# Matmul groups of the projection, gate and MLP stages draw their PSUM banks from more pools

## The chip, the cores and the metric

One core of one Trainium2 chip. The metric is the device time of one execution in microseconds; the median of three runs is compared. TensorE is PE below (its weight loads PEld), VectorE DVE, ScalarE ACT, GpSimd POOL, and SyncE, which issues every DMA, SP.

## What is computed

A sequence of 1024 tokens with 1024 features goes through two kinds of block, all in fp32.

```python
# first block, once
x = x + concat([diff_attention, neighbourhood_attention]) @ w_out
x = x + sigmoid(x @ w_ple_gate) * (p @ w_ple_proj)
# second block, layers l = 0, 1
mod = silu(c) @ w_mod[l] + b_mod[l]              # six rows of shifts, scales and gates
x = x + gt1 * (concat([dilated, latent_attention]) @ w_out_2[l])
h = rms_norm(x) * (1 + sc2) + sh2
x = x + gt2 * (square(relu(h @ w_mlp_in[l])) @ w_mlp_out[l])
```

## The kernel before

Activations are held transposed, features on partitions: a tile is 128 features by 512 tokens, and the two halves of the tokens are `half` 0 and 1. Every fp32 matrix is split into a high and a low part (`h`, `l`), and a product of a 128-feature step is three matmuls of 128x512 (`mm3`, L183 to L185; `product`, L1709). A matmul group accumulates into one PSUM bank and is then read once by DVE or ACT.

**The eight banks** belong to pools: `psG` (2 banks, tile `pg`), `psS` (2, scores, `sps`), `psA` (1, attention values, `pa`), `psT` (2, transposes, `pt`) and `psJ` (1, transposes, `pj`). A new tile of a pool waits until the reader of the tile that had the bank is done.

**The stages around the change**, by the time from the span's start:

- End of the first block, 760 to 1000 (`block1_end`). The output projection (`out_proj`) makes 16 products of 24 matmuls, for two feature tiles d by half 0, then half 1, for four pairs of d. Each is added to the old x on DVE (L872; `xo` is loaded by a DMA, two buffers), and the sum is split by ACT (L127) and DVE (L128) into the tiles a00 to a71, from which the gate's 16 products read: all eight of a half for every product. The gate's bank is read by ACT (tanh, L919), DVE adds (L920, L921). `side()` interleaves two other pieces of work: position tables (DVE L1156, `tab`, two buffers, each stored by a DMA to `acd`), and the modulation's matrix-vector sums (`mod_piece`: a DMA load `modraw`, DVE L969 into `macc`, transposes on PE into `pt` or `pj`, L161, L974).
- The output projections of the layers, near 1585 to 1700 and 3040 to 3172 (L874), behind the latent attention.
- MLP up, near 1740 to 2070 and 3200 to 3505. A feature group `fg` makes seven products of 12 matmuls (a form of Strassen's scheme): `up_first` opens x (bank S) and y (G), `up_rest` goes on with x and opens z (G). x stays open over the whole group, 19 us.
- MLP down, near 2070 to 2390 and 3515 to 3820: seven chunks `c` of two groups `dp` (`down_proj`). A group has seven products i of six matmuls for each of two columns j: x (S) takes i = 0, 2, 4, 6, y (G) i = 1 and another y i = 3, 5. After each product DVE adds the bank to x (L1831, `add_to`), so the next product into the same bank waits for that read. `u_parts` makes the chunk's operands (POOL L1812, POOL and DVE L1079, ACT L1078), `wide` its weights (a DMA load `sraw`, POOL L1684 to L1688 sums, ACT L1697, DVE and POOL L1698). The last of eight chunks is a plain product (`gemm_t`) of 16 groups.

**Order.** All engines run in order. The order of each engine's instructions is made by a list scheduler that simulates the program: among instructions that are ready in its simulation, a free bank included, it takes the one written first. So an engine's order is fixed before the run, and a bank that is free in the simulation lets a later product move ahead.

Of the kernel before, what the change touches and what calls it, by code (L numbers as in the profile page):

```python
# [11 lines left out]
F32 = mybir.dt.float32  # L12
# [6 lines left out]
P = 128  # L19
# [67 lines left out]
class Emit:  # L87
# [56 lines left out]
    def psum_g(self, shape=None):  # L144
        return self.psG.tile(shape or [P, 512], F32, tag="G", name="pg")

    def psum_s(self, shape=None):
        return self.psS.tile(shape or [P, 512], F32, tag="S", name="sps")

# [83 lines left out]
    def setup(self):  # L233
        nc = self.nc
        es = self.es
        self.dram = self.pool("dram", es, space=DRAM)
        self.const = self.pool("const", es)
        self.psS = self.pool("psS", es, {"S": 2}, PSUM)
        self.psA = self.pool("psA", es, {"A": 1}, PSUM)
        self.psT = self.pool("psT", es, {"T": 2}, PSUM)  # L240
        self.psJ = self.pool("psJ", es, {"J": 1}, PSUM)
        self.turn, self.apart = 0, False
        self.psG = self.pool("psG", es, {"G": 2}, PSUM)
        self.hp = self.pool("hp", es)
        self.wp = self.pool("wp", es, {"wh": WB, "wl": WB, "raw": 2})
        self.wring = [self.wp]
        self.st = self.pool("st", es, {"l1": 3, "l2": 3, "r24": 2, "rsy": 2, "rst": 2, "sr": 2, "stw": 2, "stc": 2, **{t: 4 for t in ("mn", "cc", "ssq", "r8")}})
        c = self.const
        self.ident = c.tile([P, P], F32, name="ident")
        make_identity(nc, self.ident)  # L250
        self.inv24 = c.tile([P, 24], F32, name="inv24")
        nc.vector.memset(self.inv24[:, 0:16], 1.0 / 64)
        nc.vector.memset(self.inv24[:, 16:24], 1.0 / 32)
        self.zeros = c.tile([P, 1], F32, name="zeros")
        nc.vector.memset(self.zeros, 0.0)
        self.mixd = [self.dram.tile([8, P, S], F32, name=f"mixd{b}") for b in range(3)]
        self.xTd = [self.dram.tile([8, P, S], F32, name=f"xTd{b}") for b in range(3)]
        self.xTm = self.dram.tile([8, P, S], F32, name="xTm")
        self.modd = {}
# [602 lines left out]
    def out_proj(self, w, b, gate, order, after, step=lambda: None, done=lambda d, half: None, pair=True):  # L862
        nc = self.nc

        def mul(d, half, wt, c0):
            sl = slice(half * 512, half * 512 + 512)
            xo = self.xt.tile([P, 512], F32, tag="xo", name="xo")
            self.dma(xo, self.xTd[b][d, :, sl])
            ps = self.psum_g()
            self.gemm_t(ps, self.mix, half, wt, 8, c0, order)  # L870
            if gate is None:
                nc.vector.tensor_tensor(self.X(d, half), ps, xo, op=OP.add)  # L872
            else:
                nc.vector.scalar_tensor_tensor(self.X(d, half), ps, gate[:, d:d + 1], xo, op0=OP.mult, op1=OP.add)  # L874
                self.dma(self.xTm[d, :, sl], self.X(d, half))
            done(d, half)

        self.halves(w, mul, after, step, self.first_w, pair)
# [9 lines left out]
    def block1_end(self, after):  # L888
        nc = self.nc
        x1 = self.act()  # L890

        def split_x(d, half):
            hi, lo = self.act_tile(x1, d, half)
            self.split(hi, lo, self.X(d, half))

        es = ExitStack()
        self.mod_pool = False
        self.mp = self.pool("mp2", es, {"mraw": 3})
        self.wring = [self.wp] * WB + [self.pool("gw", es, {"wh": 2, "wl": 2})] * 2
        self.mraw = (self.mp, "mraw")  # L900
        pp = self.pool("ple", es, {"gth": 3, "pl": 3})
        tables = self.position_tables(es)
        per = -(-len(tables) // 16)

        def side():
            for _ in range(min(per, len(tables))):
                tables.pop(0)()
            self.run_background(3)

        self.out_proj(self.A["w_out"][0], 0, None, None, lambda half: None, side, split_x, False)  # L910

        def mul(d, half, wt, c0):
            sl = slice(half * 512, half * 512 + 512)
            pl = pp.tile([P, 512], F32, tag="pl", name="ple")
            self.dma(pl, self.pled[d, :, sl])
            ps = self.psum_g()
            self.gemm_t(ps, x1, half, wt, 8, c0)
            th = pp.tile([P, 512], F32, tag="gth", name="gth")
            nc.scalar.activation(th, ps, AF.Tanh, scale=0.5)  # L919
            nc.vector.scalar_tensor_tensor(th, th, 1.0, pl, op0=OP.add, op1=OP.mult)  # L920
            nc.vector.tensor_tensor(self.X(d, half), self.X(d, half), th, op=OP.add)  # L921
            self.dma(self.xTd[1][d, :, sl], self.X(d, half))

        self.halves(self.A["w_ple_gate"][0], mul, after, side)
        self.wring = [self.wp]
        es.close()
# [792 lines left out]
    def mlp(self, l, close, after):  # L1719
# [18 lines left out]
            self.dma(ud[n, :, half * 512:half * 512 + 512], r)  # L1738

        def up_first(fg, w, pool, tag="r"):  # L1740
            x, y = self.psum_s(), self.psum_g()
            self.product(x, w, self.B, 0, slice(0, P), 4, True)
            t = keep(x)
            self.product(y, w, self.B, 1, slice(0, P), 4, True)
            put(2 * fg, 0, y, t, pool, tag)
            return x

        def up_rest(fg, w, x, up):
            mul = lambda ps, i, start: self.product(ps, w, self.B, i, slice(0, P), 4, start)
            z = self.psum_g()  # L1750
            mul(x, 2, False)
            t = keep(x)
            mul(z, 3, True)
            t5 = keep(z)
            mul(x, 4, False)
            put(2 * fg + 1, 1, x, t5, up)
            mul(z, 5, False)
            put(2 * fg, 1, z, t, up)
            mul(x, 6, False)
            put(2 * fg + 1, 0, x, None, up)  # L1760
# [72 lines left out]
        def down_proj(c, dp, B):  # L1833
            w = wide(A["w_mlp_out_2"][l], 4 * c, 2, dp * 512, 512)
            q = []
            for j in range(2):
                q.append((self.psum_s(), slice(j * P, (j + 1) * P), 4 * dp + j, 4 * dp + j + 2))
            y = {}
            for i in range(7):
                for j, (x, cols, d1, d2) in enumerate(q):  # L1840
                    if i in (1, 3):
                        y[j] = self.psum_g()
                    ps = y[j] if i in (1, 3, 5) else x
                    self.product(ps, w, B, i, cols, 2, i in (0, 1, 3))
                    for d, half in (((d1, 0),), ((d1, 0),), ((d1, 1),), ((d2, 1),), ((d2, 1),), ((d1, 1),), ((d2, 0),))[i]:
                        add_to(d, half, ps)
# [9 lines left out]
        with ExitStack() as eu:  # L1856
            up = self.pool("ud", eu, {"uq": 4})
            self.XT = {}
            B = u_parts(0, up)
            for d in (0, 2, 1, 3, 4, 6, 5, 7):  # L1860
                self.XT[d, 0], self.XT[d, 1] = self.slot(16 + d, F32)
                for half in range(2):
                    self.dma(self.X(d, half), self.xTm[d, :, half * 512:half * 512 + 512])
            for c in range(7):
                down_proj(c, 0, B)
                down_proj(c, 1, B)
                if c < 6:
                    B = u_parts(c + 1, up)
            U = {}
            for half in range(2):  # L1870
                for k in range(4):
                    u = up.tile([P, 512], F32, tag="uq", name="ul")
                    self.dma(u, ud[28 + k, :, half * 512:half * 512 + 512])
                    U[k, half] = hi, lo = self.slot(((14, 15, 24, 25), (26, 27, 8, 9))[half][k])
                    nc.scalar.copy(hi, u)
                    V.tensor_tensor(lo, u, hi.bitcast(F32), op=OP.subtract)
            wts = [self.load_w(A["w_mlp_out_2"][l, 28 * P:32 * P], [(dp * 512, 512)], 4) for dp in range(2)]
            for half in range(2):
                for d in range(8):
                    ps = self.psum_g()  # L1880
                    self.gemm_t(ps, U, half, wts[d // 4], 4, (d % 4) * P)
                    add_to(d, half, ps)
                    if l == 0:
                        self.dma(self.xTd[2][d, :, half * 512:half * 512 + 512], self.X(d, half))
                after(half)
# [80 lines left out]
```

## Time and profile before

| | us |
|---|---|
| median of three runs | 3882.95 (3879.51 to 3885.87) |
| profiled execution | 3880.11 |
| its span, first to last instruction | 3878.2 |
| PE busy in the span | 3613.2 (93%) |
| DVE busy | 2821.6 (73%) |
| POOL busy | 1565.9 (40%) |

The profiled execution ran 2.8 us below the median, and 1.9 us of it lie around the span. "Busy" is the union of an engine's instructions. In a view of waits, `PE pg L183 <- DVE xT L872` reads: PE's instruction of line 183 that writes `pg` stood idle until DVE's instruction of line 872 that writes `xT` was done. PEld waits are mostly the same idle time seen on the weight load.

### The profile page before, as it was taken

How to read it: one execution, taken by the hardware profiler on the slowest of the kernel's cores; microseconds unless marked ns; L12 is line 12 of the kernel's file. 1: busy time of each engine (PE TensorE's matmuls, PEld its weight loads, DVE VectorE, ACT ScalarE, POOL GpSimd, SP SyncE). 2: the span in 40 equal slices, each digit the busy share in tenths (PEclk: the TensorE clock that was granted, in tenths of full speed). 3: DMA queues.
4: the chain of work that ended last, by engine and by line, in shares of the span. 5: the costliest groups of instructions: out<-in, count | busy, mean ns of one | idle time of the engine just before them, and what ended most of it. 6: DMA issues, size and time to landing. Idle time of an engine off the chain costs nothing.

```text
span 3878.2 us, 59074 instructions
## 1 busy us (share of the span) xinstructions
PE 3613.2 (93%) x20508; PEld 3097.2 (80%) x20508; DVE 2821.6 (73%) x6304; ACT 1842.2 (48%) x3671; POOL 1565.9 (40%) x1317
## 2 busy tenths in 40 slices
PE   7999899989899899988998999899899998998999
PEld 6988899768899888777786777899788776886777
DVE  5888877667666788658889986666788646447885
ACT  4555555623455678533333333455677633333331
POOL 2334222322322223235337895422133235339882
PEclk9999999999899999999999999999999999999999
DMA  6322323575445500224555323455500132334322
GB/s 193 100 76 74 81 75 83 152 254 183 120 143 152 161 11 25 65 94 144 187 185 193 114 90 108 124 142 156 159 14 26 53 106 101 109 122 147 104 93 82
DMA packets 374077, 446.17 MB, mean 115 GB/s; under 512 B 50037, under 2 KB 246532, under 8 KB 373780
## 3 DMA queue, kind: packets, MB, share of 16 engines
q1 hardware_dynamic: 373780, 442.41, 36.7%
q8 instruction: 162, 2.65, 0.3%
q14 instruction: 135, 1.11, 0.1%
HBM read 312.17 MB, written 101.54 MB: 107 GB/s over the span
## 4 chain that ended last, share of the span: by engine, by line
PE 59%; DVE 16%; POOL 8%; DMA 8%; issue 5%; ACT 4%; SPq 1%; DVEq 0%; ACTq 0%; POOLq 0%
PE pg L183 8%; PE pg L184 8%; PE pg L185 8%; PE sps L1709 8%; PE pg L1709 6%; PE sps L459 2%; PE pt L155 2%; PE pt L693 2%; PE sps L460 2%; DVE macc L969 2%; PE sps L183 2%; DMA modraw<-in_w_mod_dram 2%; PE sps L184 2%; PE pa L700 2%; PE sps L185 2%
## 5 line engine op out<-in xcount | busy, mean ns | idle before, releaser
L209 POOL TENSOR_TENSOR wl<-raw,wh 128x512 fp32r<-128x512 f32 (+2 forms) x234 | 302.5, 1304 | 578.0 <-ACT wh L208 492.7
L128 DVE TENSOR_TENSOR pl<-pt,ph 128x512 fp32r<-128x512 f32 (+3 forms) x406 | 267.6, 665 | 85.8 <-ACT ph L127 77.3
L127 ACT CAST ph<-pt 128x512 fp32r<-128x512 f32 (+3 forms) x406 | 226.0, 574 | 136.1 <-PE pt L693 52.3
L208 ACT CAST wh<-raw 128x512 fp32r<-128x512 f32 (+2 forms) x234 | 138.1, 611 | 221.4 <-DMA raw<-in_w_out_dram 69.5
L969 DVE SCALAR_TENSOR_TENSOR macc<-modraw,csil,macc 128x256 f32<-128x256 f32 x280 | 205.3, 733 | 47.9 <-DMA modraw<-in_w_mod_dram 43.2
L459 PE MATMUL sps<-ks,qs 128*128 128x512 f32 (+3 forms) x480 | 195.8, 410 | 18.5 <-DVE mn L493 10.3
L1698 DVE TENSOR_TENSOR wl<-ssum,wh 128x1024 fp32r<-128x1024 f32 x116 | 168.6, 1453 | 47.5 <-ACT wh L1697 47.5
L1697 ACT CAST wh<-sraw 128x1024 fp32r<-128x1024 f32 x116 | 97.0, 836 | 221.8 <-PE sps L1709 121.4
L1684 POOL TENSOR_TENSOR ssum<-sraw 128x512 f32<-128x512 f32 x58 | 79.0, 1362 | 288.6 <-DVE wl L1698 122.7
L407 POOL TENSOR_TENSOR qn<-qn,r 128x512 f32<-128x512 f32 x64 | 68.8, 1080 | 266.5 <-DVE r L122 109.6
L460 PE MATMUL sps<-kl,qs 128*128 128x512 f32 (+3 forms) x480 | 175.4, 367 | 0.0
L1697 ACT CAST wh<-ssum 128x1024 fp32r<-128x1024 f32 x116 | 121.4, 1047 | 108.9 <-PE pg L1709 79.4
L1643 ACT ACTIVATE xm<-xm,mn 128x1024 f32<-128x1024 f32 x128 | 148.4, 1159 | 32.6 <-DVE mn L493 32.5
L493 DVE CUSTOM_DVE_ANT_0 xd<-sps,dtab 128x256 f32<-128x256 f32 (+1 forms) x256 | 103.3, 412 | 80.1 <-PE sps L460 72.0
L459 PEld LDWEIGHTS sps<-ks,qs 128*128 128x128 f32 x480 | 108.2, 225 | 28.5 <-DVE mn L493 15.0
L1698 POOL TENSOR_TENSOR wl<-sraw,wh 128x512 fp32r<-128x512 f32 x58 | 87.4, 1507 | 90.0 <-ACT wh L1697 81.4
L1698 DVE TENSOR_TENSOR wl<-sraw,wh 128x1024 fp32r<-128x1024 f32 x58 | 94.4, 1628 | 32.0 <-ACT wh L1697 23.9
L700 PE MATMUL pa<-pl,vpm 128*128 128x512 f32 x256 | 109.2, 427 | 2.9 <-DVE pl L128 2.7
L460 PEld LDWEIGHTS sps<-kl,qs 128*128 128x128 f32 x480 | 110.8, 231 | 1.3
L699 PE MATMUL pa<-ph,vpm 128*128 128x512 f32 x256 | 109.2, 427 | 0.6 <-ACT ph L127 0.2
L493 DVE CUSTOM_DVE_ANT_0 xm<-sps,zeros,mn 128x512 f32<-128x512 f32 x128 | 95.3, 745 | 13.8 <-PE sps L185 12.3
L693 PE MATMUL pt<-ident,xm 128*128 128x128 f32 x688 | 104.6, 272 | 0.6 <-DVE pl L128 0.6
(1483 smaller groups left out, 13960.6 us busy)
## 6 DMA issues: line engine op xcount, KB each, us to landing
modraw<-in_w_mod_dram SPq DMA_DIRECT2D x192, 256.0 KB
ud<-r SPq DMA_DIRECT2D x128, 256.0 KB
sraw<-in_w_mlp_in_dram SPq DMA_DIRECT2D x60, 512.0 KB
sraw<-in_w_mlp_out_dram SPq DMA_DIRECT2D x56, 512.0 KB
raw<-in_w_in_dram SPq DMA_DIRECT2D x194, 128.0 KB
uq<-ud SPq DMA_DIRECT2D x96, 256.0 KB
ks<-khh SPq DMA_DIRECT2D x128, 128.0 KB
dtab<-awd SPq DMA_DIRECT2D x32, 512.0 KB
```

The source lines that it names most:

```text
L127: nc.scalar.copy(hi, src)
L128: nc.vector.tensor_tensor(lo, src, hi.bitcast(F32), op=OP.subtract)
L183: nc.tensor.matmul(ps, lh, rh, start=start, stop=False)
L184: nc.tensor.matmul(ps, lh, rl, start=False, stop=False)
L185: nc.tensor.matmul(ps, ll, rh, start=False, stop=stop)
L209: nc.gpsimd.tensor_tensor(wl[:, sl], raw, wh[:, sl].bitcast(F32), op=OP.subtract)
L459: nc.tensor.matmul(ps, self.Q[m][:, q], self.K[m][:, k], start=True, stop=False)
L460: nc.tensor.matmul(ps, self.Q[m][:, q], self.KL[m][:, k], start=False, stop=True)
L969: nc.vector.scalar_tensor_tensor(acc, raw[:, k], c, acc, op0=OP.mult, op1=OP.add)
L1697: nc.scalar.copy(wh[:, 0:m], x)
L1698: (nc.vector if i < 3 else nc.gpsimd).tensor_tensor(wl[:, 0:m], x, wh[:, 0:m].bitcast(F32), op=OP.subtract)
L1709: nc.tensor.matmul(ps, x[:, k, cols], y, start=start and k + n == 0, stop=(k, n) == (nk - 1, 2), skip_group_check=True)
```

## The change

The matmul groups of six places no longer take a fixed pool but the next of a turn: output projections, gate and the last MLP chunk G, S, G, S, A (`psum_w()`); x of the MLP S, S, T; y and z of the MLP G, G, A. The counters run on over the whole program. No instruction is added or removed, and the pools keep their sizes. The `plain` products at the head of the MLP keep S and G.

```diff
+    def psum_w(self, turn="GSGSA"):
+
+        n = self.wide[turn] = self.wide.get(turn, -1) + 1
+        return {"G": self.psum_g, "S": self.psum_s, "A": self.psum_a, "T": self.psum_one}[turn[n % len(turn)]]()
+
+    def psum_one(self):
+        return self.psT.tile([P, 512], F32, tag="T", name="pt")
...
-        self.turn, self.apart = 0, False
+        self.turn, self.apart, self.wide = 0, False, {}
...
@@ out_proj
-            ps = self.psum_g()
+            ps = self.psum_w()
             self.gemm_t(ps, self.mix, half, wt, 8, c0, order)
...
@@ block1_end (the gate)
-            ps = self.psum_g()
+            ps = self.psum_w()
             self.gemm_t(ps, x1, half, wt, 8, c0)
...
@@ mlp: up_first, up_rest
-            x, y = self.psum_s(), self.psum_g()
+            x, y = self.psum_w("SST"), self.psum_w("GGA")
...
-            z = self.psum_g()
+            z = self.psum_w("GGA")
...
@@ mlp: down_proj
-                q.append((self.psum_s(), slice(j * P, (j + 1) * P), 4 * dp + j, 4 * dp + j + 2))
+                q.append((self.psum_w("SST"), slice(j * P, (j + 1) * P), 4 * dp + j, 4 * dp + j + 2))
...
-                        y[j] = self.psum_g()
+                        y[j] = self.psum_w("GGA")
...
@@ mlp: the last chunk
-                    ps = self.psum_g()
+                    ps = self.psum_w()
                     self.gemm_t(ps, U, half, wts[d // 4], 4, (d % 4) * P)
```

## Rows read from the trace of the kernel before

**Rows 1.** Busy time by stage; columns: PE, PEld, DVE, ACT, POOL busy, clock, DMA.
```profile
760.00:883.00 123.00, 105.15 (x452) 84.85 (x451) 85.45 (x164) 35.29 (x62) 31.03 (x24) 0.93 0.74 238
883.00:1000.00 117.00, 106.53 (x497) 88.57 (x496) 86.08 (x177) 39.11 (x64) 37.24 (x30) 0.94 0.51 165
1585.00:1700.00 115.00, 112.51 (x550) 91.78 (x549) 48.73 (x96) 46.15 (x80) 33.86 (x29) 1.00 0.33 108
...
3230.00:3515.00 285.00, 282.83 (x1244) 233.51 (x1243) 138.63 (x141) 101.49 (x146) 121.30 (x87) 1.00 0.40 135
3515.00:3820.00 305.00, 276.12 (x1155) 215.44 (x1155) 246.89 (x277) 105.07 (x153) 262.19 (x173) 0.99 0.29 97
```

**Rows 2.** Waits from 760 to 890; then DVE's groups from 760 to 883.
```profile
DVE tab L1156 <- DMA acd<-tab: 23.1, 14, 4.4
...
PE pg L183 <- DVE xT L872: 16.2, 5, 7.8
...
L1156 DVE SCALAR_TENSOR_TENSOR tab<-cmult,ac 128x512 f32<-128x512 f32 x32 | 25.7, 810 | 25.0 <-DMA acd<-tab 23.1 <-ACT ac L1151 1.7
L872 DVE TENSOR_TENSOR xT<-pg,xo 128x512 f32<-128x512 f32 x16 | 10.9, 682 | 0.9 <-DMA xo<-xTd 0.9
```

**Rows 3.** Timeline, projection to gate: DVE (L128), then PE (L183).
```profile
872.98 0.68 DVE L128 TENSOR_TENSOR a70l<-xT,a70h 128x512 fp32r<-128x512 f32 x1
...
886.19 1.78 DVE L128 TENSOR_TENSOR a71l<-xT,a71h 128x512 fp32r<-128x512 f32 x1
...
879.25 0.39 PE L183 MATMUL pg<-a00h,wh 128*128 128x512 f32 x1
...
890.38 0.39 PE L183 MATMUL pg<-a01h,wh 128*128 128x512 f32 x1
...
895.82 0.39 PE L183 MATMUL pg<-a01h,wh 128*128 128x512 f32 x1
```

**Rows 4.** PE's timeline behind one wait for a bank; the clock of two stretches.
```profile
860.93 0.50 PE L183 MATMUL pg<-a00h,wh 128*128 128x512 f32 x1 [1.97 <-DVE xT L872]
...
864.18 0.63 PE L184 MATMUL pg<-a30l,wh 128*128 128x512 f32 x1
864.61 0.63 PE L185 MATMUL pg<-a30h,wl 128*128 128x512 f32 x1
...
820.00:830.00 10.00, 7.74 (x28) 5.93 (x27) 7.05 (x10) 1.24 (x2) 3.71 (x3) 0.83 0.70 215
...
860.00:870.00 10.00, 9.07 (x34) 7.30 (x35) 9.82 (x19) 5.09 (x9) 2.73 (x2) 0.83 0.83 264
```

**Rows 5.** PE's idle moments at layer 0's projection, and at the second layer's head.
```profile
1628.49 0.66 PE L155 MATMUL pt<-ident,oT 128*128 128x128 f32 x4 [0.68 <-ACT oT L702]
1630.26 0.74 PE L183 MATMUL pg<-a60h,wh 128*128 128x512 f32 x2 [0.67 <-ACT a60h L127]
1632.74 0.50 PE L183 MATMUL pg<-a01h,wh 128*128 128x512 f32 x1 [0.39 <-DVE xT L874]
...
2435.72 0.36 PE L183 MATMUL pg<-wh,a00h 128*128 128x256 f32 x1 [0.95 <-DVE b22l L1831]
```

**Rows 6.** Waits of five down chunks, 3569.8 to 3787.7; busy time of one.
```profile
POOL ssum L1684 <- DMA sraw<-in_w_mlp_out_dram: 20.4, 5, 6.0
...
PE sps L1709 <- DVE b16h L1831: 11.4, 5, 2.4
...
3613.78:3656.90 43.12, 40.26 (x169) 32.34 (x169) 35.18 (x41) 15.27 (x23) 39.89 (x27) 0.96 0.30 94
```

**Rows 7.** Chain of work inside that chunk: start, length, what.
```profile
3631.17 1.26 POOL wl L1698
...
3632.45 0.38 SPq L108
...
3632.88 4.77 DMA sraw<-in_w_mlp_out_dram
...
3637.81 1.32 POOL ssum L1684
```

**Rows 8.** PE's timeline where the wait of rows 6 arises.
```profile
3607.18 0.39 PE L1709 MATMUL pg<-a21h,wh 128*128 128x512 f32 x1
...
3609.91 0.39 PE L1709 MATMUL sps<-a01h,wh 128*128 128x512 f32 x1
...
3613.78 0.79 PE L1709 MATMUL sps<-a41h,wh 128*128 128x512 f32 x1 [2.36 <-DVE b16h L1831]
```

**Rows 9.** DVE reading both pools' banks at L1831; PE's wait for weights, layer 0 up.
```profile
L1831 DVE SCALAR_TENSOR_TENSOR b16h<-pg,mod,b16h x16: 737/750/751, 2071.8 to 3825.6; 128x512 f32<-128x512 f32 x16
...
L1831 DVE SCALAR_TENSOR_TENSOR b16h<-sps,mod,b16h x14: 737/739/742, 2069.9 to 3786.9; 128x512 f32<-128x512 f32 x14
...
PE sps L1709 <- ACT wh L1697: 2.1, 1, 2.1
```

## The prediction

> **What bounds the kernel now.** I read the busy time by stage first, because the change touches only some stages and each has its own limit [rows 1]. Three kinds show. In MLP up of layer 1 PE is busy 282.83 of 285 us: there is nothing for a bank to free. In the projection of layer 0 it is 112.51 of 115. In the end of the first block (105.15 of 123) and in MLP down (276.12 of 305) PE has idle time, 18 and 29 us. So the question is who ends those idle stretches, and the waits answer it.
>
> In the end of the first block PE's one large wait is for a bank: 16.2 us in five waits of line 183 for the add of line 872 that reads the bank [rows 2]. Two banks hold two finished products, and DVE is late with its adds. It is late because it runs in order and stands 23.1 us before the tables of L1156, whose two buffers are still being stored. DVE itself hardly waits for PE or for anything else at its adds: 0.9 us before L872. The stage is thus paced by DVE and the table stores; PE's wait is the result.
>
> In MLP down the most visible PE wait comes once per chunk, 11.4 us in five, for the add into b16h [rows 6]. The plan put the products of y (a21) ahead of those of x, since x's bank was still taken; so i = 2 of x (a41) comes right behind i = 0 (a01) and must wait for its read, 2.36 us [rows 8]. It looks like a bank shortage. But POOL is busy 39.89 of that chunk's 43.12 us, and what idles it is its own loop: its L1698 releases the weight buffer, SP issues the load, it takes 4.77 us, and POOL's L1684 starts behind it [rows 7]. That wait is 20.4 us in five chunks [rows 6]. PE is not in that loop.
>
> **The change part by part.** No instruction is added, so the sum has only waits and order in it. DVE reads a bank of G in 750 ns and one of S in 739 at the same line [rows 9]; I take 0 for the change of pool, between 11 ns less and 11 more per read, and the same for T and A, which this line never reads now.
>
> *End of the first block.* With five banks PE may run up to four products past the last unread one. A product takes 895.82 - 890.38 = 5.44 us [rows 3], so three more banks are 16 us more of lead than now, more than any single wait (7.8 the longest), and all 16.2 us of waiting for L872 can go. What is late next is DVE. The gate needs all of half 0's splits, and the last, a70l, ends at 872.98 + 0.68 = 873.7; PE starts the gate at 879.25 [rows 3]. If DVE does the same work in the same order, the first product of the gate can end at 874.4 (three matmuls behind a70l), the second at 874.4 + 5.4 = 879.8, and the third waits for a71l at 886.19 + 1.78 = 888.0 and ends at 888.7. Before, it ended at 895.8. From there PE runs on as before. **Gain 7.1 us**, out of 16.2. The bounds: 0, if the gate's own DVE work, 86.08 of 117 us [rows 1], gives it back; and if the plan also brings the adds forward on DVE, all 16.2 plus the slow matmuls behind the waits. After the 1.97 us wait PE's matmuls come 0.43 us apart, the 1.2 GHz level, where a product's 24 in 5.44 us are 0.227 apart, the 2.4 GHz level [rows 3, 4]. Some 15 such matmuls cost 3 us, and two stretches of the stage have the mean clock 0.83 [rows 4], so 6: 22 us in all. SP's queue is not changed by itself: each product still issues one `xo` load behind the add two before it, and those adds come no later. The weights of the next pair need buffers that PE frees, and it frees them earlier.
>
> *Layer projections.* At the end of latent attention PE stands 0.68, 0.67 and 0.39 us [rows 5]. The last is for a bank and goes. In the first two a third product could be started, but its fourth step needs the same a60h. I take half of 1.35: 1.1 us a layer, 2.2 in both, between 0 and 3.5. That the first product of layer 1 draws A, which the last attention values hold, costs nothing while G and S products can be moved ahead of it.
>
> *Head of the second layer.* The 0.95 us wait for the bank that L1831 reads [rows 5] goes, since the last chunk's groups now lie in G, S and A: 1.0 us, between 0 and 1.
>
> *MLP up.* 0: PE has no idle time in layer 1 [rows 1]. What hides the reads of one bank there are the products into the others; if that cover were gone, each read would cost PE some 0.75 us [rows 9].
>
> *MLP down.* With T for x the next group's i = 0 need not wait for the last group's read, the pulled order of rows 8 goes, and with it PE's 2.36 us. I count 0: while POOL paces the chunk, PE then waits for POOL's operands instead. The bounds are the rival below, and the same amount lost if the new order suits POOL worse.
>
> Sum: 7.1 + 2.2 + 1.0 = 10.3 us. Against the profiled execution 3880.1 - 10.3 = 3869.8; the median lies 2.8 us above that execution, so **3872 us**, 0.28% less. A measurement of this kernel tells about 0.2%, 7.8 us, from no change.
>
> **A rule weighed.** In the down chunks the trace shows the same PE gap in each chunk and a POOL that is 92% busy [rows 6]. The Trainium skill's page Perfetto Trace Analysis, section Identifying Performance Opportunities, says that a gap which repeats on the engine that should be saturated can mean that there is not enough SBUF or PSUM for the next tile. By it the change would win the gap itself, which is the first rival; by the row the gap only shows POOL's pace.
>
> **The rivals.**
>
> *The down gap was worth its length.* If the planner, no longer short of banks, also orders POOL, ACT and DVE better, each of ten steady chunks could lose up to POOL's idle time, 43.12 - 39.89 = 3.2 us, and one and a half more where the clock falls behind the wait (0.96 in that chunk, 4% of 43 us = 1.7). At 2.3 to 4 us a chunk: 23 to 40 us, so 3832 to 3849. For it: DVE's late add sits behind its own weight splits, whose order the plan decides. Against it: rows 7. Chance 0.2.
>
> *DVE takes it all.* The tables and modulation sums move with the adds, the gate's start stays at 879, and only the small terms are left: 3880 to 3883. For it: DVE does not wait for PE today. Against it: PE starts the gate 5.6 us after its last operand of half 0 is ready, which is PE's own lateness. Chance 0.2.
>
> *Slower: PE stands before weights in MLP up.* With three banks for x the plan can pull the next group's first product ahead of the present group's last ones. PE is in order: if its weights land later than the plan thinks, everything of the present group stands behind it. The one such wait now is 2.1 us, for ACT's split [rows 9]. If it comes in 10 of 28 groups (the third that holds T), that is 21 us lost, less the 10 gained: 3893. It decides from a lateness of more than the product that is passed over, 2.7 us of cover. Against it: PE waits for weights once in layer 0's stage and hardly in layer 1, so they come with time to spare. Chance 0.15.
>
> **How the numbers follow.** My forecast has 0.45 and its own range is 3862 to 3880 (the bounds 22 + 4.5 and 0, with most near DVE's unchanged order). Faster by over 0.2% means under 3875.2: two thirds of the forecast's case (0.30), the down rival (0.20) and a little of the DVE rival (0.04): 0.54. Slower means over 3890.7: most of the slower rival, a little less the cases where its waits are short: 0.14. The rest, 0.32, is the same. The range runs from 3840, inside the down rival, to 3888, leaving out the ends of both.
>
> **What would show it.** Right: in the profile after, no wait of PE for L872; the gate's first matmul near 870 to 875 and its third product ending near 889; PE's idle time before the gate now put down to L128 or L127; the down chunks still 43 us long with POOL near 40 busy, the b16h wait gone or moved to POOL's parts. Wrong: chunks of 41 us or less (the first rival), the gate's third product still ending near 896 (the second), or new PE waits for L1697 or L1698 in MLP up with its groups longer than 19 us (the third).

## The result and the profile after

The changed kernel takes 3906.69 us in the median of four runs (3905.58 to 3910.88), the kernel before 3882.56 us beside it: ratio 1.0064, 95% interval 1.0047 to 1.0081, 24 us slower. The forecast was 3872. The profiled execution has a span of 3905.6 us where it was 3878.2. In the changed kernel's rows every line number above 150 is 8 higher (the bank's add of L872 is L880, the product's matmul L1709 is L1717, the macc of L969 is L977).

First, where the 27.4 us arise. I followed marks that both traces have. The end of the first block (ACT's last tanh) moves from 971.5 to 972.0, the first `keep` of layer 0's MLP up from 1731.6 to 1732.7: nothing yet. The `keep` copies that bracket MLP up of layer 0 then tell it. Of the kernel before, in a view by tile (engine, out and in, count: shortest/median/longest ns, first to last start):

```profile
L1727 ACT COPY keep<-sps x30: 561/589/590, 1731.6 to 2053.7; 128x512 f32<-128x512 f32 x30
L1727 ACT COPY keep<-pg x15: 572/578/592, 1773.1 to 2061.2; 128x512 f32<-128x512 f32 x15
```

And of the changed kernel:

```profile
L1735 ACT COPY keep<-sps x20: 562/584/611, 1732.7 to 2087.2; 128x512 f32<-128x512 f32 x20
...
L1735 ACT COPY keep<-pt x10: 571/580/589, 1813.2 to 2105.9; 128x512 f32<-128x512 f32 x10
L1735 ACT COPY keep<-pa x5: 583/590/594, 1822.2 to 2106.4; 128x512 f32<-128x512 f32 x5
```

The stage grew from 329.6 to 373.7 us, 44 us, more than the whole loss. From its end to the first keep of layer 1 the changed kernel gets back 14 us (1117.9 where it was 1132.0); MLP up of layer 1 is as long as before (312.0 and 310.8); from its end to the span's end it gets back 5 (369.3 and 374.2). With the 1.1 us of the beginning: 1 + 44 - 14 + 1 - 5 = 27.

What ended PE's idle time there stands in PE's waits from 1735 to 2115. Kernel before (us in total, times, longest):

```profile
PE pj L155 <- DVE macc L969: 8.8, 3, 4.7
...
PE pt L155 <- DVE macc L969: 2.3, 1, 2.3
PE sps L1709 <- ACT wh L1697: 2.1, 1, 2.1
```

Changed kernel:

```profile
PE pt L163 <- DVE macc L977: 26.7, 5, 11.2
PE sps L1717 <- ACT wh L1705: 6.3, 6, 2.1
...
PE pj L163 <- DVE macc L977: 4.1, 2, 2.4
...
PE sps L1717 <- DVE wl L1706: 3.1, 4, 1.6
```

The new wait is not one of a product at all. It is the transposes of the modulation sums into `pt`, standing before their macc. The timeline of PE at the longest one shows why products suffer (start, length, what, idle before it):

```profile
1878.36 0.39 PE L1717 MATMUL pg<-a70h,wl 128*128 128x512 f32 x1
1878.59 0.38 PE L163 MATMUL pt<-ident,macc 128*128 128x128 f32 x2
1890.14 0.66 PE L163 MATMUL pt<-ident,macc 128*128 128x128 f32 x2 [11.18 <-DVE macc L977]
1890.45 0.78 PE L1717 MATMUL pt<-a00h,wh 128*128 128x512 f32 x1
1891.03 0.63 PE L1717 MATMUL pt<-a00l,wh 128*128 128x512 f32 x1
1891.45 0.63 PE L1717 MATMUL pt<-a00h,wl 128*128 128x512 f32 x1
```

Directly behind the second sum comes the first product of a group whose x lies in T. The same order, a sum in T directly ahead of an x in T, stands at 1963.18 and 2039.40, where PE waits 3.02 and 9.70 us for the macc. And DVE in the same stretch:

```profile
1872.38 0.48 DVE L977 SCALAR_TENSOR_TENSOR macc<-modraw,csil,macc 128x256 f32<-128x256 f32 x1
1879.01 0.42 DVE L169 TENSOR_REDUCE sr<-pt 128x2 f32<-128x256 f32 x1 [6.15 <-PE pt L163]
1879.35 1.32 DVE L975 TENSOR_SCALAR macc<-modraw,csil 128x256 f32<-128x256 f32 x1
...
1880.70 1.52 DVE L977 SCALAR_TENSOR_TENSOR macc<-modraw,csil,macc 128x256 f32<-128x256 f32 x3
1884.04 1.01 DVE L977 SCALAR_TENSOR_TENSOR macc<-modraw,csil,macc 128x256 f32<-128x256 f32 x2 [1.81 <-DMA modraw<-in_w_mod_dram]
1888.99 1.00 DVE L977 SCALAR_TENSOR_TENSOR macc<-modraw,csil,macc 128x256 f32<-128x256 f32 x2 [3.95 <-DMA modraw<-in_w_mod_dram]
```

DVE ends the macc at 1889.99 and PE starts 0.15 us later; DVE itself stood before the loads of `w_mod` (`modraw`), 5.76 us in two waits. Over the whole window this wait of DVE doubles, kernel before and then changed kernel:

```profile
DVE macc L969 <- DMA modraw<-in_w_mod_dram: 25.7, 20, 4.7
```

```profile
DVE macc L977 <- DMA modraw<-in_w_mod_dram: 49.3, 31, 4.2
```

The loads are only a part of the 11.18 us. The macc of the second sum begins at 1879.35, because DVE, in order too, had stood 6.15 us before PE's transposes of the first sum. `modraw` has two buffers, and SP issues the next load when DVE has read one: behind the macc of 1872.38 one goes out at 1872.88, and the next not before 1881.21, behind the first of the three of 1880.70. So PE, DVE and the loads wait for each other in a ring, and with the two sums side by side in PE's queue no product covers it.

So the theory is this. The two banks of T go round in the order in which the program asks for them. The sums of a group are written after it (`run_background(8)`) and two of three of them take T; the next x that takes T must have its bank after them, so its product stands behind them in PE's in-order queue. Before, x had banks that no sum uses, and a late sum could be left for later while products went on. The windows of MLP up show the price (columns as in [rows 1]); kernel before:

```profile
1740.00:2060.00 320.00, 302.44 (x1285) 244.62 (x1284) 269.33 (x357) 105.26 (x153) 136.00 (x93) 0.95 0.54 175
```

Changed kernel:

```profile
1740.00:2060.00 320.00, 268.68 (x1095) 211.64 (x1096) 250.26 (x352) 87.44 (x128) 114.18 (x77) 0.91 0.48 155
```

PE is busy 34 us less in the same stretch, and slower too: the mean clock falls from 0.95 to 0.91, since the matmuls behind a wait come 0.43 us apart (1891.03, 1891.45), the 1.2 GHz level, instead of 0.227.

The steps of the forecast have their rows after as well. The end of the first block, in windows and then in waits from 760 to 890, against [rows 1, 2]:

```profile
760.00:883.00 123.00, 113.21 (x494) 91.33 (x494) 87.55 (x162) 41.18 (x76) 34.81 (x26) 0.96 0.73 236
883.00:1000.00 117.00, 103.02 (x481) 85.35 (x482) 93.15 (x186) 37.70 (x63) 35.55 (x30) 0.93 0.55 176
```

```profile
DVE tab L1164 <- DMA acd<-tab: 11.6, 10, 2.9
...
PE pt L163 <- DVE macc L977: 3.2, 1, 3.2
...
PE pg L191 <- DVE xT L880: 2.9, 1, 2.9
```

PE's wait for the bank is nearly gone, 2.9 us where it was 16.2, and PE is 8 us busier in the first window; but it is 3.5 us less busy in the second, and the last tanh is not earlier.

MLP down, the five steady chunks of layer 1 between the same two adds; kernel before, then changed kernel:

```profile
3569.80:3787.70 217.90, 200.98 (x840) 157.74 (x840) 175.99 (x200) 73.99 (x108) 195.93 (x130) 0.98 0.29 96
```

```profile
3594.40:3812.10 217.70, 200.56 (x835) 159.34 (x834) 176.82 (x199) 75.11 (x108) 195.21 (x129) 0.97 0.29 97
```

They are as long as before, to 0.2 us in 218. PE's wait for the add into b16h, 11.4 us before [rows 6], is gone, with other waits in its place, and POOL hardly stands before its loads now. PE's longest waits and POOL's for its loads there, changed kernel:

```profile
PE sps L1717 <- ACT b25h L1086: 2.8, 1, 2.8
PE pg L1717 <- ACT a51h L1086: 2.7, 1, 2.7
PE sps L1717 <- DVE b22l L1839: 2.2, 1, 2.2
...
POOL ssum L1692 <- DMA sraw<-in_w_mlp_out_dram: 1.5, 1, 1.5
```

### The profile page after: what moved, and what is told of

Read it like the earlier page. It is cut to its first block, busy times and chain, and to the rows that moved or that the text cites. A ratio compares the mean times of both kernels' runs of the same rounds, so it can differ in the third digit from the quotient of the medians.

```text
span 3905.6 us, 58999 instructions
## 1 busy us (share of the span) xinstructions
PE 3626.5 (93%) x20508; PEld 3112.2 (80%) x20508; DVE 2820.3 (72%) x6304; ACT 1839.3 (47%) x3671; POOL 1565.0 (40%) x1317
## 4 chain that ended last, share of the span: by engine, by line
PE 58%; DVE 18%; DMA 8%; POOL 7%; issue 5%; ACT 3%; SPq 1%; DVEq 0%; ACTq 0%; POOLq 0%
PE pg L191 6%; PE pg L193 6%; PE pg L192 6%; PE sps L1717 5%; PE pg L1717 4%; PE sps L191 3%; PE sps L192 3%; PE sps L193 3%; DMA modraw<-in_w_mod_dram 3%; PE pt L1717 2%; PE pt L701 2%; PE sps L467 2%; DVE macc L977 2%; PE pt L163 2%; PE pa L1717 2%
## 5 line engine op out<-in xcount | busy, mean ns | idle before, releaser
L128 DVE TENSOR_TENSOR pl<-pt,ph 128x512 fp32r<-128x512 f32 (+3 forms) x406 | 267.2, 665 | 90.3 <-ACT ph L127 77.9
L977 DVE SCALAR_TENSOR_TENSOR macc<-modraw,csil,macc 128x256 f32<-128x256 f32 x280 | 179.4, 641 | 74.1 <-DMA modraw<-in_w_mod_dram 69.4
L1706 DVE TENSOR_TENSOR wl<-ssum,wh 128x1024 fp32r<-128x1024 f32 x116 | 178.1, 1537 | 55.2 <-ACT wh L1705 55.1
L1705 ACT CAST wh<-sraw 128x1024 fp32r<-128x1024 f32 (+1 forms) x116 | 96.8, 835 | 243.6 <-PE sps L1717 79.1
L1705 ACT CAST wh<-ssum 128x1024 fp32r<-128x1024 f32 x116 | 121.6, 1049 | 158.1 <-PE pt L1717 55.4
L1692 POOL TENSOR_TENSOR ssum<-sraw 128x512 f32<-128x512 f32 x58 | 83.0, 1431 | 273.6 <-DVE wl L1706 133.5
L1706 POOL TENSOR_TENSOR wl<-sraw,wh 128x512 fp32r<-128x512 f32 x58 | 87.8, 1514 | 99.1 <-ACT wh L1705 99.1
L1695 POOL TENSOR_TENSOR ssum<-sraw 128x512 f32<-128x512 f32 x58 | 84.8, 1462 | 59.4 <-DVE wl L1706 49.1
L545 ACT ACTIVATE x<-x,mn 128x1024 f32<-128x1024 f32 x64 | 73.8, 1154 | 65.6 <-DVE mn L501 65.3
```

Source lines behind the costliest of these rows:

```text
L128: nc.vector.tensor_tensor(lo, src, hi.bitcast(F32), op=OP.subtract)
L977: nc.vector.scalar_tensor_tensor(acc, raw[:, k], c, acc, op0=OP.mult, op1=OP.add)
L1705: nc.scalar.copy(wh[:, 0:m], x)
L1706: (nc.vector if i < 3 else nc.gpsimd).tensor_tensor(wl[:, 0:m], x, wh[:, 0:m].bitcast(F32), op=OP.subtract)
```

## The experiments

Each ratio is against the kernel before on the same chip, run in turns with it. Lengths of stages are from one profile each. "Up" below is MLP up of layer 0 from first to last keep.

**x of MLP up back on S.**

```diff
-            x, y = self.psum_w("SST"), self.psum_w("GGA")
+            x, y = self.psum_s(), self.psum_w("GGA")
```

> The changed kernel, but x of MLP up draws S alone again (x of MLP down keeps S, S, T). Theory A (x in T stands in PE's order behind the modulation sums that share T's two banks, and these are late): MLP up of layer 0, first to last keep, falls from 374 us back to about 330, the first chunk of layer 0's down part takes back some 15 of it, and the end comes 26 to 30 us earlier: about 3878. Theory B (the planner loses the time for another reason: y and z in A, or PE before weights): little changes, 3900 to 3907.

Measured: 3869.55 us, ratio 0.9961 (0.9945 to 0.9977). Up is 319.3 us. Both are below what theory A gave. PE's wait of the sums in T is nearly gone, in the same view as above:

```profile
PE pj L163 <- DVE macc L977: 5.4, 1, 5.4
...
PE pt L163 <- DVE macc L977: 2.2, 2, 1.6
```

One word of the change turns the sign. The loss is all in x's bank in MLP up, and what is left of the change is a gain.

**The sums on J, x still over S, S, T.**

```diff
+                self.apart = True
                 self.run_background(8)
+                self.apart = False
```

> The changed kernel, but the modulation sums that are issued during MLP up take the bank J alone, so that T has only x in it there; x keeps its turn S, S, T. Theory A: the tie between x and the sums is gone, MLP up of layer 0 falls from 374 us to 330 to 335, and the kernel ends near 3878, as with x on S. Rival C (a third bank for x is itself bad: the plan pulls x ahead of its weights or of other products): up stays near 374 and the time near 3905. If the sums, now in one bank, hold each other up instead, something between.

Measured: 3868.89 us, ratio 0.9954 (0.9937 to 0.9971); up is 322.6 us, both again below theory A. x has ten of its copies out of `pt`, as in the changed kernel, and nothing is lost:

```profile
L1735 ACT COPY keep<-pt x10: 574/587/589, 1808.4 to 2054.9; 128x512 f32<-128x512 f32 x10
L1735 ACT COPY keep<-pa x5: 570/578/579, 1823.1 to 2061.3; 128x512 f32<-128x512 f32 x5
```

So a third bank for x does no harm (rival C falls). What does harm is sharing T with the sums.

**The kernel before with x of MLP up over S, S, T alone.**

```diff
-            x, y = self.psum_s(), self.psum_g()
+            x, y = self.psum_w("SST"), self.psum_g()
```

> The kernel before with one part of the change alone: x of MLP up turns over S, S, T. Theory A: this part carries the loss, so MLP up of layer 0 grows from 330 to about 374 us, half or so of the excess over 28 comes back in the first down chunk, and the time is about 3910 (27 to 30 us more than before). Theory B: 3880 to 3886.

Measured: 3918.04 us, ratio 1.0083 (1.0066 to 1.0101), 32 us more where theory A had 27 to 30; up is 367.7 us, and the wait is back:

```profile
PE pt L163 <- DVE macc L977: 24.6, 5, 7.6
PE pj L163 <- DVE macc L977: 7.5, 4, 3.0
```

This one line alone costs more than the whole change. Taken away, cut at the other end, and put in alone, the tie gives the same answer three times.

**The sums without their loads.** The changed kernel; in MLP up (`still` is set around `run_background(8)` alone) the sums read a constant tile, so that part of the modulation is not computed.

```diff
-        raw = self.mraw[0].tile(...)
-        self.dma(raw, self.A["w_mod_2"][...])
+        raw = self.ones if self.still else self.mraw[0].tile(...)
+        self.still or self.dma(raw, self.A["w_mod_2"][...])
```

> The changed kernel, x of MLP up over S, S, T and the sums in T and J as there, but in MLP up the modulation sums read a constant tile: their loads of w_mod are left out, while DVE's operations, the transposes and the reads of the banks stay. If the sums are late because of their loads (DVE stood 49.3 us before them), they now come in time, PE hardly waits for macc, MLP up of layer 0 falls from 374 us to between 311 (layer 1, which has no sums) and 330, and the time to about 3860 to 3880. If they are late because DVE comes to them late in its own order, up stays over 350 and the time over 3890.

Measured: 3874.46 us, ratio 0.9969 (0.9957 to 0.9980); up is 335.2 us, 5 above the band expected. Of PE's waits for macc from 1735 to 2115 one is left (lines 3 higher again):

```profile
PE pt L163 <- DVE macc L980: 7.4, 1, 7.4
```

The order stays: a sum in T still stands directly ahead of the next x in T, but PE no longer stops there, as here and at 1943.09:

```profile
1882.37 0.38 PE L163 MATMUL pt<-ident,macc 128*128 128x128 f32 x2
1882.51 0.48 PE L1720 MATMUL pt<-a00h,wh 128*128 128x512 f32 x1
```

38 of the 44 us go with the loads: the sums are late in the main because `modraw` is. The wait that is left, at 2009.30, has two sums side by side again, and DVE's own operations on the second between them. The run also takes load off the DMA engines (their share in MLP up falls from 0.48 to 0.30), so some of the 38 may be weights that land earlier; the waits for weights are small in both (PE for L1705 and L1706 9.4 us in the changed kernel, 6.6 here for the same two lines).

**The last MLP chunk on G.** After PE's last projection matmul (the last of L193, in the last chunk) the changed kernel needs 15.5 us to the end, where it was 7.4: the copies of the store (L1911) had been interleaved with the last products and now come in a row.

```diff
-                    ps = self.psum_w()
+                    ps = self.psum_g()
                     self.gemm_t(ps, U, half, wts[d // 4], 4, (d % 4) * P)
```

> The changed kernel, but the last MLP chunk of each layer draws its banks from G alone again. Theory D (with five banks the plan puts all products of the last chunk ahead of the transposes of the store, so that these are left for the end): the stretch from PE's last projection matmul to the end falls from 15.5 us to about 7.4, and the time to about 3898 (8 us less than the changed kernel). Rival: the transposes are late because they wait for the sums on DVE, which come 8 us later in any case: no change, 3906.

Measured: 3909.98 us, ratio 1.0065 (1.0051 to 1.0080): no change. The copies spread out again, as theory D says; changed kernel, then this one:

```profile
L1911 ACT COPY oo<-pt x6: 586/586/587, 3891.0 to 3899.3; 128x512 f32<-128x512 f32 x6
```

```profile
L1911 ACT COPY oo<-pt x6: 585/590/592, 3867.6 to 3901.1; 128x512 f32<-128x512 f32 x6
```

The tail falls to 7.7 us, but PE's last projection matmul moves from 3890.1 to 3899.0: the order changed and the sum did not. Theory D saw a true thing and priced it wrongly, and its rival named the wrong reason.

**One part at a time on the kernel before.** Four kernels, on one chip.

First block (output projection and gate over G, S, G, S, A):

```diff
-            ps = self.psum_g()
+            ps = self.psum_w() if gate is None else self.psum_g()
...
-            ps = self.psum_g()
+            ps = self.psum_w()
             self.gemm_t(ps, x1, half, wt, 8, c0)
```

> The kernel before with the turn G, S, G, S, A in the first block's output projection and gate alone. The prediction's step (PE starts the gate earlier, its third product ends near 889): the gate's last tanh some 7 us earlier than 971.5, the time 7 us less. Theory E (DVE with its tables and splits sets the gate's end, and PE's time saved at the banks is only waited elsewhere): last tanh at 971 to 975, first keep of MLP up up to 4 us later, the time the same within 4 us.

Measured: ratio 0.9995 (0.9985 to 1.0006). Last tanh at 974.1. The interval leaves room for 5.8 us of gain, so the 7 us are not there, and theory E's forecast holds. The tanh by itself couldn't decide it: it lies at 970.8 to 981.7 in the eight profiles with the old first block and at 972.0 to 976.8 in the six with the new one. That DVE sets the gate's end is theory E's reason and is not shown by this run.

MLP down alone:

```diff
-                q.append((self.psum_s(), ...
+                q.append((self.psum_w("SST"), ...
...
-                        y[j] = self.psum_g()
+                        y[j] = self.psum_w("GGA")
```

> The kernel before with the turns of MLP down alone (x over S, S, T; y over G, G, A; the last chunk stays on G). The prediction's step: 0, the steady chunks stay 43 us long. Its first rival: 2.3 to 4 us in each of ten chunks, 23 to 40 us. By the runs with x of MLP up on S, the down part of layer 1 gives some 3 to 5 us in all and that of layer 0 nothing: 3 to 5 us less.

Measured: 3880.89 against 3885.97 us, ratio 0.9984 (0.9973 to 0.9995): 5 us less in the medians, 6 by the ratio. From layer 1's last keep to the end it is 370.6 us; the kernel before has 374.2, and 373.4 in a second profile. The steady chunks are not shorter; the first product of the last chunk comes 311.2 us behind the last keep where it was 317.3. The place is not certain by that: with y and z of MLP up alone, which leaves MLP down as it was, these two stretches are 370.7 and 313.8 us.

y and z of MLP up alone:

```diff
-            x, y = self.psum_s(), self.psum_g()
+            x, y = self.psum_s(), self.psum_w("GGA")
...
-            z = self.psum_g()
+            z = self.psum_w("GGA")
```

> The kernel before with y and z of MLP up over G, G, A alone; x stays on S. The prediction's step: 0, since PE has no idle time in MLP up. Theory F (that is so in layer 1 alone; layer 0's up has idle time, and the third bank takes some 10 us of it, as it seems in the run with x on S, 319 us from first to last keep where it was 330): 8 to 11 us less, all of it in layer 0's up, layer 1's unchanged at 311.

Measured: ratio 0.9996 (0.9985 to 1.0007). Theory F falls. Up is 321.7 us here, but three kernels that leave MLP up alone have 322.1, 324.6 and 323.2.

The layers' output projections alone:

```diff
-            ps = self.psum_g()
+            ps = self.psum_g() if gate is None else self.psum_w()
             self.gemm_t(ps, self.mix, half, wt, 8, c0, order)
```

> The kernel before with the turn G, S, G, S, A in the output projections of the two layers alone. The prediction's step: 2.2 us less. By the trace of the changed kernel, where layer 0's projection ends 2.7 us later and its first add comes 15 us later: the same within 3 us, since PE is the bound there and the order among its products changes nothing in their sum.

Measured: 3877.80 us, ratio 0.9978 (0.9968 to 0.9989): 8.5 us less, more than either number expected. In layer 0 the stretch from the last tanh to the first keep falls from 760.1 to 756.7 us. At the head of the projection the two idle moments before L183 of [rows 5] are gone; one of the three is left:

```profile
1641.95 0.66 PE L163 MATMUL pt<-ident,oT 128*128 128x128 f32 x4 [0.68 <-ACT oT L710]
```

That places some 3.4 us of the 8.5, or 4.4 against the second profile of the kernel before (761.1); the idle moments that are gone sum to only 1.1. In the changed kernel they are gone too, but the stretch is 760.7 us: there the gain doesn't show at these marks. The rest I could not place: in layer 1 the stretch from the last down product to the first keep is as long as before (803.3 and 803.8).

**The two gaining parts together**, projections and down, each edit as above, the rest as in the kernel before.

> The kernel before with the two parts that gained by themselves: the layers' output projections (ratio 0.9978 alone) and MLP down (0.9984 alone). If these two carry all that the change gains, their sum is 0.9962, 14 us less than the kernel before, as much as the changed kernel gave with x of MLP up back on S (0.9961). If the parts get in each other's way, or one of them was luck, it lies between 0.998 and 1.

Measured: 3866.18 against 3881.07 us, ratio 0.9964 (0.9954 to 0.9974). The parts add up, and this version beats both kernels.

**The sums on J, with the first block and the last chunk on G.**

> The changed kernel with the modulation sums of MLP up on J alone, and the first block and the last MLP chunk on G again. Theory A: with the tie cut, a third bank for x costs nothing and gains nothing, so 0.9955 to 0.9965, as the sums on J with everything else. If the third bank for x is worth something by itself, under 0.995.

Measured: 3865.50 us, ratio 0.9968 (0.9955 to 0.9980). The ratio lies just above the band that theory A gave, 0.9955 to 0.9965, and the interval covers that band without reaching 0.995: the third bank for x gains nothing that shows.

**A control.**

> The kernel before once more, as a control for the length of MLP up in layer 0, first to last keep: 329.6 us in the profile shown, 322 to 325 in three kernels that leave it alone. If it is noise of the loads, 320 to 330; if the kernel before is really longer there than those three, 328 to 331.

Measured: up is 326.5 us, 3 less than in the profile shown. That is in the first band and not in the second: this stage differs by some us from one execution to the next, and the 10 us of theory F were read from one profile against another. The last tanh lies at 978.6 here, 7 us later than in the profile shown. Against such differences the loss stands out: of the fourteen profiles, the three in which x shares T with loaded sums have 367.7 to 375.3 us in up, the ten without that tie 319.3 to 329.6, and the one without the loads 335.2.

## Why the prediction was wrong

*MLP up: 0.* This is the step that failed, and with it the sign. It reads: "0: PE has no idle time in layer 1", and what hides the bank's reads is the products into the others. For layer 1 that held (312.0 us, from 310.8). But I took the row of layer 1 for both layers; in layer 0 PE was busy 302.44 of 320 us. Layer 0's up carries the modulation sums and layer 1's doesn't. The three facts were all in front of me: T belongs to `psum_t`, from which the sums draw; DVE waits for `modraw` in that stage; all engines run in order. I asked whether the new banks would be free, and not whose work would now have to be done first. Measured: +44 us in the stage, of which 14 come back by layer 1's up, which fits sums that are done earlier (the last macc at 2092 instead of 2155); put in alone, x's turn costs 32 us in the end.

*The slower rival* had the right stage and the right form: every third group, that with x in T, everything behind it on an in-order PE. It named weights as the late operand. These waits rose only from 2.1 to 9.4 us. The late operand was macc, and the price, 21 us, was half of what the stage lost.

*End of the first block: 7.1 us.* The mechanism ran as described up to a point: the wait for L872 went from 16.2 to 2.9 us, and PE starts the gate's first product at 873.2, inside the 870 to 875 given. From there the step failed. It said "from there PE runs on as before". The third product starts at 889.32 and ends before 894.77, where the next one begins, against the 888.7 that I gave and the 895.82 of before. PE does less in between: in the middle of the second product it stands 3.24 us before a sum's transposes, and the matmuls behind that come at the lower clock:

```profile
884.27 0.41 PE L163 MATMUL pt<-ident,macc 128*128 128x128 f32 x2 [3.24 <-DVE macc L977]
```

The last tanh lies at 972.0, within the 970.8 to 981.7 of the profiles with the old first block; alone this part is 0.9995, so at most 5.8 us. The rival "DVE takes it all" has the outcome right, hardly any gain, but not the way: it kept the gate's start at 879, and the start moved.

*Layer projections: 2.2 us.* The idle moments went as described, but the size was wrong: alone the part gives 8.5 us (4 to 12), where my range for both layers ended at 3.5. Of these 3.4 are seen in layer 0; what gives the rest is open.

*Head of the second layer: 1.0 us.* In the changed kernel PE's wait for the read of L1839 (L1831 before) is gone there, but a wait of 2.4 us for a split (DVE L1029) is new; with the last chunk back on G the ratio hardly moves (1.0065 from 1.0064), so the term doesn't show.

*MLP down: 0.* Right for the steady chunks (217.7 us for five, from 217.9), but not for the reason given. POOL is busy 195 us in both, which fits POOL as their pace; yet its wait for its own loads, the loop of [rows 7], fell from 20.4 us to 1.5, as the plan changed, and the chunks are no shorter, since POOL now stands before other tiles. What holds a chunk at 43 us is thus not shown. The rival that gave 23 to 40 us is excluded. Outside these chunks, where I did not look, the part gives some 6 us. The rule of the Trainium skill that the prediction weighed (Perfetto Trace Analysis, Identifying Performance Opportunities) named this very gap: a repeated gap as a sign of too little PSUM. The measurement decides against it for these chunks: this gap went and they are no shorter.

The parts without x's turn sum to 10.3 us in my working, and to 15 in the runs (0.9961). That they are so near is luck: the first block gave hardly any of its 7.1, and the projections and MLP down gave what I had not counted. But x's turn decided the sign alone. The Trainium skill's Perfetto Trace Analysis says, in Matmul Optimizations, that all eight PSUM banks should be used. Here the banks had all been in use, and the run with x alone in T is 0.83% slower: which work shares a bank counted for more than how many banks a product may draw.

What stays open: why the plan puts the sums ahead of x rather than x ahead of the sums was not tried, nor whether a third buffer for `modraw` would do as well as a bank of its own for the sums. That the planner expects the loads of `w_mod` sooner than they land fits DVE's waits, but is argued, not shown.

## What to carry to other kernels

Before a product is given a bank from another pool, list who else draws from that pool and what those tiles wait for: in an in-order queue the shared pool ties the fast work to the slowest of its users. Check this in every stage where the pool's other users are active, not in the stage with the cleanest row. And measure the parts of a change alone: here one part lost 32 us and hid 15 us of gain in two others.

## What I had not expected

Loads whose sums no product of the stage reads can hold up PE: in one stretch of 11.18 us of idle time DVE stood 5.76 us before two `modraw` loads, and this reached PE by way of a transpose of 0.66 us and a shared bank. A wait also costs more than its length, as the granted clock of the whole stage fell from 0.95 to 0.91. And moving the store's transposes from between the last products to behind them made no difference that could be measured (1.0065 and 1.0064), though the tail of the trace looked 8 us worse.
